# A two-layer decoder trunk on one core: sums of a Strassen weight piece queued ahead of its last two splits, and three folds of the second token tile queued behind the held weight pairs

## The chip, the cores and the metric

The kernel runs on one core of one Trainium2 chip, as one launch. The metric is device time in microseconds (us). The figure for a kernel is the median of several runs; a profiled execution has a time of its own, beside the span from its first to its last traced instruction.

## What is computed

The reference is a decoder trunk of two layers over 256 tokens of width 1024, in float32. Each layer is a half-step feed-forward block, a mixer with two gated branches, and a second half-step feed-forward block, each followed by a layer norm:

```python
def _swiglu(x, w1, w3, w2):
    return (jax.nn.silu(x @ w1) * (x @ w3)) @ w2
...
    for l in range(DEPTH):
        h = _swiglu(x, ffn_w1[l, 0], ffn_w3[l, 0], ffn_w2[l, 0])
        x = _layernorm(ALPHA * x + 0.5 * h, ln_g[l, 0], ln_b[l, 0])
        h = _mixer(x, l, w_in[l], gate_b[l], sgu_ln_g[l], sgu_ln_b[l], sgu_w[l], sgu_b[l],
                   lam[l], diff_ln_g[l], w_branch[l], w_out[l], cos, sin)
        x = _layernorm(ALPHA * x + h, ln_g[l, 1], ln_b[l, 1])
        h = _swiglu(x, ffn_w1[l, 1], ffn_w3[l, 1], ffn_w2[l, 1])
        x = _layernorm(ALPHA * x + 0.5 * h, ln_g[l, 2], ln_b[l, 2])
    return x
```

The change lies in the product with `w2` (2816 x 1024), which is done four times: twice in each of the two layers.

## The kernel before

**Tiling.** The 256 tokens are two token tiles of 128 (`t` = 0, 1), and the 1024 output columns are two halves of 512 (`c` = 0, 1). A product with a weight is kept at float32 accuracy by splitting: the weight block `raw` is copied to a rounded `hi` on ScalarE (ACT), and VectorE (DVE) makes `lo = raw - hi`; the left operand is split in the same way, and TensorE (PE) sums hi by hi, lo by hi and hi by lo (`three`, L214). So every weight block passes a chain: one transfer of 1 MB into `raw` (four buffers, issued from SP's queue), one `hi` on ACT, one `lo` on DVE (eight buffers each), then PE. A plain weight piece gives two halves of 128x1024 each (`stream`, `whi` at L172, `wlo` at L174).

**The product with w2.** The 22 row blocks of 128 of `w2` are taken in pairs. Four pairs (`SQ`) go through one Strassen step: seven products instead of eight, into seven PSUM banks `S[1]` to `S[7]`. The other seven pairs (`PQ`) are plain. The order on PE is: Strassen piece 0, plain pair, piece 1, plain pair, piece 2, plain pair, piece 3, and then four plain pairs whose splits are made but whose matmuls are held back (`held`). The held matmuls come last, for (t, c) = (0,0), (0,1), (1,0), (1,1), and within each for the four pairs in turn: 6 matmuls a pair, 24 for each (t, c).

**A Strassen piece** (`stream_s`, L284 to L319) loads one `raw` of four blocks of 512 columns. Four splits (`cut`; `shi` at L296, `slo` at L298) make the operands: `a` (512 columns, product 1), `b` (products 3 and 2), and, after sums of blocks are written back into `raw`, `c` (products 5 and 7) and `d` (products 6 and 4). The sums are three DVE instructions: L309 (1024 columns, needed by `c`), L311 and L312 (512 columns each, needed by `d`). PE takes the products in the order 1, 2, 5, 6, 3, 7, 4.

**The folds.** After piece 3 the seven products are combined and added into the residual tiles `xtok` (`ln.more`, seen as L477 and L479 on `xtok`, with `u` at L667 and `v` at L668): two adds for the first token tile (`xtok_143`: `S[1]`, `v`) and four for the second (`xtok_144`: `S[7]`, `v`, `u`, `S[7]` again). Then each held bank is added (`ln.part`, L486), followed by the statistics of the layer norm (L491, L498), the scaling of the row (L502) and PE transposes for the next stage (L546).

**What sets the order.** PE's order is written out by hand. The other engines run in order too, in the order that the scheduler of the programming layer gives them when the program is built; it goes by the order in the code, by a priority and by its own estimate of readiness. `behind(ins)` asks that an instruction is queued after a given one; `latest[1]` is the last lo split of the newest activations.

Of the kernel before, what the change touches and what calls it, by code (L numbers as in the profile page):

```python
# [17 lines left out]
ALU = mybir.AluOpType  # L18
# [38 lines left out]
def trunk(ctx, tc, x, xT, w13a, w13b, w2s, w2p, wb, wqk, wa, wbr, wo, gateb, sgug, sgub, sguwT, sgubias, lam, diffg,  # L57
          lng, lnb, lngT, lnbT, cosT, sinT, out):
    nc = tc.nc
    V, A, G, PE = nc.vector, nc.scalar, nc.gpsimd, nc.tensor  # L60
# [15 lines left out]
    def name(s):  # L76
        serial[0] += 1
        return f"{s}_{serial[0]}"
# [32 lines left out]
    def step():  # L111
        chunk[0] += 1
        tc.cur_priority = chunk[0] * STEP
# [33 lines left out]
    latest, added, emptied, silu, turned_by = [None, None], [None], [None], [None], [None]  # L147

    def behind(ins):

        return tc.issue_after(ins) if ins is not None else nullcontext()

    def stream(src, width=CH, sub=HC, lent=(), after=(None, None)):

        step()
        raw = raw_pool.tile([P, CH], F32, tag="raw", name=name("raw"))
        nc.sync.dma_start(raw[:, :width], src)
        out = []  # L160
        for o in range(0, width, HC):
            if o // HC in lent:
                hi, lo = ([act.tile([P, 512], F32R, tag="slot", name=name(n)) for _ in range(2)] for n in ("lhi", "llo"))
                at = [(hi[j], lo[j]) for j in range(2)]
            else:
                hi = hi_pool.tile([P, HC], F32R, tag="hi", name=name("whi"))
                lo = lo_pool.tile([P, HC], F32R, tag="lo", name=name("wlo"))
                at = [(hi[:, p : p + sub], lo[:, p : p + sub]) for p in range(0, HC, sub)]
            for p, (h, w) in zip(range(0, HC, sub), at):
                r = raw[:, o + p : o + p + sub]  # L170
                with behind(latest[0]):
                    A.activation(h, r, AF.Copy)  # L172
                with behind(after[o // HC] or latest[1]):
                    V.tensor_tensor(out=w, in0=r, in1=h.bitcast(F32), op=ALU.subtract)  # L174
            out.append((hi, lo))
        return out
# [78 lines left out]
    def rows_p(ps, t, q, piece, xh, xl, c0=0, n=512, stop=False, start=False):  # L255

        for j, k in enumerate(q):
            wh, wl = (v[:, j * 512 + c0 : j * 512 + c0 + n] for v in piece)
            three(ps[:, :n], xh(k)[:, t * P : (t + 1) * P], xl(k)[:, t * P : (t + 1) * P], wh, wl,
                  start and j == 0, stop and j == 1)  # L260
        beat(n / 1024)
# [21 lines left out]
    def stream_s(src, pair):  # L283

        step()
        raw = raw_pool.tile([P, CH], F32, tag="raw", name=name("raw"))
        nc.sync.dma_start(raw, src)

        def two():
            return hi_pool.tile([P, HC], F32R, tag="hi", name=name("shi")), lo_pool.tile([P, HC], F32R, tag="lo", name=name("slo"))  # L290

        def cut(p, o, n):
            h, w = (v[:, p[2] : p[2] + n] for v in p[:2])
            r = raw[:, o : o + n]
            with behind(latest[0]):
                A.activation(h, r, AF.Copy)  # L296
            with behind(latest[1]):
                V.tensor_tensor(out=w, in0=r, in1=h.bitcast(F32), op=ALU.subtract)  # L298

        a = (*pair, 0) if pair else None  # L300
        if a is None:
            pair = two()
            a, keep = (*pair, 0), pair
        else:
            a, keep = (*pair, 512), None
        b, c, d = ((*two(), 0) for _ in range(3))
        cut(a, 0, 512)
        cut(b, 1024, 1024)
        V.tensor_tensor(out=raw[:, :1024], in0=raw[:, :1024], in1=raw[:, 512:1536], op=ALU.add)  # L309
        cut(c, 0, 1024)  # L310
        V.tensor_tensor(out=raw[:, 1024:1536], in0=raw[:, :512], in1=raw[:, 1024:1536], op=ALU.add)  # L311
        V.tensor_tensor(out=raw[:, 1536:], in0=raw[:, 1024:1536], in1=raw[:, 1536:], op=ALU.add)  # L312
        cut(d, 1024, 1024)

        def at(p, j):
            return tuple(v[:, p[2] + j * 512 : p[2] + j * 512 + 512] for v in p[:2])

        return keep, {1: at(a, 0), 3: at(b, 0), 2: at(b, 1), 5: at(c, 0), 7: at(c, 1), 6: at(d, 0), 4: at(d, 1)}
# [246 lines left out]
    def ffn(l, f, i, norm, last=False):  # L565
# [77 lines left out]
        pair, held, plain = None, [], list(PQ)  # L643

        def plain_pair(hold):
            q = plain.pop(0)
            w = stream(w2p[l, f, PQ.index(q)])
            if hold:
                held.append((q, w))
                return  # L650
            for c in range(2):
                for t in range(NT):
                    for ps, o, m in ends[t, c]:
                        rows_p(ps, t, q, w[c], hh, hl, o, m, start=q == PQ[0] and t + c == 2)

        for n, q in enumerate(SQ):
            pair, w = stream_s(w2s[l, f, n], pair)
            for b in (1, 2, 5, 6, 3, 7, 4):
                three(S[b], *s_op[q][b], *w[b], n == 0, n == NS - 1 and b in (1, 5, 6, 7))
            beat(1.75)  # L660
            if n < NS - 1:
                plain_pair(False)
# [4 lines left out]
        V.tensor_tensor(out=u, in0=u, in1=S[1], op=ALU.add)  # L667
        V.tensor_tensor(out=v, in0=S[5], in1=u, op=ALU.subtract)  # L668
        ln.more(0, 1, v, ALU.add, ln.scale)
        ln.more(1, 1, v, ALU.add, ln.scale)  # L670
        ln.more(1, 0, u, ALU.add)
        ln.more(1, 1, S[7], ALU.add)
        while plain:
            plain_pair(True)
        for t in range(NT):
            for c in range(2):
                for ps, o, n in ends[t, c]:
# [230 lines left out]
    for l in range(DEPTH):  # L908
        norm = ffn(l, 0, 0, norm)
        norm = mixer(l, 1, norm)  # L910
        norm = ffn(l, 1, 2, norm, last=l == DEPTH - 1)
# [89 lines left out]
```

## Time and profile before

| | |
|---|---|
| median of 3 runs | 1233.25 us (1232.46 to 1234.97) |
| the profiled execution: time, span | 1233.15 us, 1231.4 us |
| DVE busy | 935.2 us (76%) |
| ACT busy | 804.0 us (65%) |
| POOL busy | 87.3 us (7%) |
| bytes moved | 252.28 MB, mean 205 GB/s |
| ACT `shi` L296 waiting for DVE `raw` L312 | 39.1 us in 16 waits |
| DVE `slo` L298 waiting for ACT `shi` L296 | 27.5 us in 21 waits |

The share of busy time is a mean over all stages. PE matmuls are pipelined: one of 512 columns has a recorded duration of some 390 ns, while the next starts some 227 ns after it, so PE time is read from the distance between starts, and a stall is a distance that is longer. Idle time of DVE or ACT costs something only where PE then waits.

### The profile page before, as it was taken

What the parts mean: (1) busy time and instruction counts of PE and PEld (TensorE: products, weight loads), DVE (VectorE), ACT (ScalarE), POOL (GpSimd) and SP (SyncE); (2) the same over time, 40 slices, a digit from 0 to 9 for tenths busy, and PEclk for the clock granted to TensorE, in tenths of its full rate; (3) what the DMA queues carried; (4) which work ended last, traced back from release to release, by engine and by line L of the source; (5) the groups of instructions that cost most, each with busy time, mean ns of one, the idle gap of its engine ahead of it and who ended that gap; (6) DMA issues with size and microseconds to landing.
All of it is one profiled execution on the core that took longest, in us unless ns stands there. A gap on an engine that the chain in (4) does not pass through costs nothing.

```text
span 1231.4 us, 16550 instructions
## 1 busy us (share of the span) xinstructions
PE 1215.8 (99%) x6045; PEld 1022.6 (83%) x6045; DVE 935.2 (76%) x1504; ACT 804.0 (65%) x1316; POOL 87.3 (7%) x184
## 2 busy tenths in 40 slices
PE   9999999999999999999999999999999999999997
PEld 8888878888888888888788888788888888888885
DVE  6657997886587985679974779979767879657795
ACT  6677666679665565776556776467885654776760
POOL 0100000234100000000000000002440000000000
PEclk9999999999999999999999999999999999999999
DMA  8985665654744657666756756565556356668540
GB/s 316 315 260 175 236 238 175 212 173 161 258 173 151 239 178 249 202 176 227 251 176 234 209 184 239 205 216 189 177 185 226 138 190 222 224 198 240 172 173 35
DMA packets 82338, 252.28 MB, mean 205 GB/s; under 512 B 47521, under 2 KB 48593, under 8 KB 55633
## 3 DMA queue, kind: packets, MB, share of 16 engines
q1 hardware_dynamic: 78288, 238.31, 57.5%
q0 software_dynamic: 3536, 12.13, 3.0%
q8 instruction: 47, 0.77, 0.2%
q10 hardware_dynamic: 432, 0.79, 0.2%
q14 instruction: 35, 0.28, 0.1%
HBM read 235.47 MB, written 1.05 MB: 192 GB/s over the span
## 4 chain that ended last, share of the span: by engine, by line
PE 58%; issue 22%; DVE 12%; ACT 5%; DMA 2%; POOL 1%; DVEq 0%; ACTq 0%; POOLq 0%
PE bank L214 19%; PE sbank L214 16%; PE bank L226 12%; PE bank L233 6%; DVE wlo L174 3%; DVE slo L298 3%; PE bank L385 2%; ACT shi L296 1%; ACT columns L601 1%; PE sbank L734 1%; DVE xtok L479 1%; ACT whi L172 1%; DVE raw L312 1%; DMA bc<-in_lng 1%; DVE hlo L180 1%
## 5 line engine op out<-in xcount | busy, mean ns | idle before, releaser
L174 DVE TENSOR_TENSOR wlo<-raw,whi 128x1024 fp32r<-128x1024 f32 (+1 forms) x410 | 450.7, 1117 | 161.6 <-ACT whi L172 118.0
L172 ACT ACTIVATE whi<-raw 128x1024 fp32r<-128x1024 f32 (+1 forms) x410 | 387.0, 968 | 192.5 <-PE sbank L214 67.9
L214 PE MATMUL bank<-whi,x 128*128 128x512 f32 x840 | 264.7, 391 | 0.0
L214 PEld LDWEIGHTS bank<-whi,x 128*128 128x128 f32 x840 | 157.8, 188 | 32.5
L214 PE MATMUL bank<-wlo,x 128*128 128x512 f32 x420 | 163.6, 390 | 0.0
L214 PE MATMUL sbank<-whi,x 128*128 128x512 f32 x512 | 158.9, 389 | 0.0
L226 PE MATMUL bank<-x,whi 128*128 128x512 f32 x640 | 158.4, 396 | 0.0
L226 PEld LDWEIGHTS bank<-x,whi 128*128 128x128 f32 x640 | 116.6, 188 | 25.9 <-issue 2.6
L214 PEld LDWEIGHTS sbank<-whi,x 128*128 128x128 f32 x512 | 96.1, 188 | 19.9
L214 PE MATMUL sbank<-wlo,x 128*128 128x512 f32 x256 | 99.7, 389 | 0.0
L296 ACT ACTIVATE shi<-raw 128x1024 fp32r<-128x1024 f32 (+1 forms) x64 | 58.9, 945 | 56.9 <-DVE raw L312 39.1
L214 PEld LDWEIGHTS bank<-wlo,x 128*128 128x128 f32 x420 | 78.9, 188 | 16.0
L298 DVE TENSOR_TENSOR slo<-raw,shi 128x1024 fp32r<-128x1024 f32 (+1 forms) x64 | 68.8, 1088 | 27.5 <-ACT shi L296 27.5
L233 PE MATMUL bank<-x,wlo 128*128 128x256 f32 x640 | 85.8, 285 | 0.0
L233 PEld LDWEIGHTS bank<-x,wlo 128*128 128x128 f32 x640 | 81.5, 191 | 2.3
L214 PE MATMUL sbank<-whi,hhi 128*128 128x512 f32 x168 | 66.4, 395 | 0.0
L214 PE MATMUL sbank<-wlo,hhi 128*128 128x512 f32 x168 | 66.2, 394 | 0.0
L214 PE MATMUL sbank<-whi,hlo 128*128 128x512 f32 x168 | 66.0, 393 | 0.0
L234 ACT ACTIVATE r<-bank 128x256 f32<-128x256 f32 x112 | 41.8, 379 | 27.6 <-PE bank L233 27.6
L552 ACT ACTIVATE xf<-sbank,ln_b,ln_g 128x128 f32<-128x128 f32 x80 | 30.0, 455 | 40.8 <-PE sbank L546 40.8
L214 PEld LDWEIGHTS sbank<-wlo,x 128*128 128x128 f32 x256 | 48.1, 188 | 10.0
L445 POOL DMA_DIRECT2D bc<-in_lng x6 | 3.2, 530 | 712.9 <-DVE bc L444 712.9
(233 smaller groups left out, 1938.7 us busy)
## 6 DMA issues: line engine op xcount, KB each, us to landing
raw<-in_w13b SPq DMA_DIRECT2D x76, 1024.0 KB, 5.4
raw<-in_w2p SPq DMA_DIRECT2D x28, 1024.0 KB, 4.9
raw<-in_wa SPq DMA_DIRECT2D x24, 1024.0 KB, 5.3
raw<-in_w2s SPq DMA_DIRECT2D x16, 1024.0 KB, 4.9
raw<-in_wb SPq DMA_DIRECT2D x16, 1024.0 KB, 4.9
raw<-in_wqk SPq DMA_DIRECT2D x16, 1024.0 KB, 4.8
raw<-in_wbr SPq DMA_DIRECT2D x16, 1024.0 KB, 4.8
raw<-in_w13a SPq DMA_DIRECT2D x8, 1024.0 KB, 4.8
```

The costliest lines, as they stand in the source:

```text
L172: A.activation(h, r, AF.Copy)
L174: V.tensor_tensor(out=w, in0=r, in1=h.bitcast(F32), op=ALU.subtract)
L180: return a.ins, V.tensor_tensor(out=lo, in0=src, in1=hi.bitcast(F32), op=ALU.subtract).ins
L214: PE.matmul(ps, xx, w, start=start and n == 0, stop=stop and n == 2)
L226: PE.matmul(b[-1], hi[:, k * P : (k + 1) * P], xc(k), start=k == 0, stop=False)
L233: PE.matmul(b[n][:, :T], lo[:, k * P : (k + 1) * P], xc(k)[:, :T], start=False, stop=k == KT - 1)
L234: emptied[0] = A.activation(r[:, s], b[n][:, T:], AF.Copy, scale=scale).ins
L296: A.activation(h, r, AF.Copy)
L298: V.tensor_tensor(out=w, in0=r, in1=h.bitcast(F32), op=ALU.subtract)
L312: V.tensor_tensor(out=raw[:, 1536:], in0=raw[:, 1024:1536], in1=raw[:, 1536:], op=ALU.add)
L385: PE.matmul(ps[t][m], x[:, j, o + t * P : o + (t + 1) * P], y, start=k0 + j == 0 and o == 0 and y is hi, stop=k0 + j == KT - 1 and y is lo)
L552: A.activation(xf[:, s], b[:, s], AF.Identity, scale=self.gT[:, f], bias=self.bT[:, f])
```

## The change

Two places are written in another order. In `stream_s` the three sums are all written ahead of the splits `c` and `d`, and both lo splits of these two are asked to be queued behind the last sum. In `ffn` the loop that streams the four held pairs is written ahead of the last three folds of the second token tile. No instruction is added or removed, and the arithmetic is the same.

```diff
-        def cut(p, o, n):
+        def cut(p, o, n, after=None):
             h, w = (v[:, p[2] : p[2] + n] for v in p[:2])
             r = raw[:, o : o + n]
             with behind(latest[0]):
                 A.activation(h, r, AF.Copy)
-            with behind(latest[1]):
+            with behind(after or latest[1]):
                 V.tensor_tensor(out=w, in0=r, in1=h.bitcast(F32), op=ALU.subtract)
...
         V.tensor_tensor(out=raw[:, :1024], in0=raw[:, :1024], in1=raw[:, 512:1536], op=ALU.add)
-        cut(c, 0, 1024)
         V.tensor_tensor(out=raw[:, 1024:1536], in0=raw[:, :512], in1=raw[:, 1024:1536], op=ALU.add)
-        V.tensor_tensor(out=raw[:, 1536:], in0=raw[:, 1024:1536], in1=raw[:, 1536:], op=ALU.add)
+        last = V.tensor_tensor(out=raw[:, 1536:], in0=raw[:, 1024:1536], in1=raw[:, 1536:], op=ALU.add).ins
+        cut(c, 0, 1024, last)
         cut(d, 1024, 1024)
...
         ln.more(0, 1, v, ALU.add, ln.scale)
+        while plain:
+            plain_pair(True)
         ln.more(1, 1, v, ALU.add, ln.scale)
         ln.more(1, 0, u, ALU.add)
         ln.more(1, 1, S[7], ALU.add)
-        while plain:
-            plain_pair(True)
```

In the built program PE's order and the queues of SP and POOL are unchanged; DVE's order changes, and ACT's in two kinds of places.

On DVE, in piece 3 of the first of the four products with `w2`, the rows run before as follows; `slo_1438` is the lo of split `b`, `slo_1440` of `c`, `slo_1442` of `d`, and L311 and L312 are the two sums that `d` needs.

```order
L298 TENSOR_TENSOR slo_1438<-raw_1435,shi_1437 128x1024
L298 TENSOR_TENSOR slo_1440<-raw_1435,shi_1439 128x1024
L311 TENSOR_TENSOR raw_1435<-raw_1435 128x512
L312 TENSOR_TENSOR raw_1435<-raw_1435 128x512
L298 TENSOR_TENSOR slo_1442<-raw_1435,shi_1441 128x1024
```

The same place after the change (in the new line numbers the two sums are L310 and L311):

```order
L298 TENSOR_TENSOR slo_1438<-raw_1435,shi_1437 128x1024
L310 TENSOR_TENSOR raw_1435<-raw_1435 128x512
L311 TENSOR_TENSOR raw_1435<-raw_1435 128x512
L298 TENSOR_TENSOR slo_1440<-raw_1435,shi_1439 128x1024
L298 TENSOR_TENSOR slo_1442<-raw_1435,shi_1441 128x1024
```

The lo split of `c` now stands behind the two sums, directly ahead of that of `d`. Pieces 0 and 1 change alike; in piece 2 the scheduler had other work between these rows, and only their order changes.

Next on DVE come the folds and the splits of the held pairs. Before, from the end of the first fold group to the first held bank; `wlo_1513` is the second half of the third held pair, `wlo_1519` and `wlo_1523` are the two halves of the fourth:

```order
L668 TENSOR_TENSOR v_1476<-bank_1206,u_1475 128x512
L477 TENSOR_TENSOR xtok_144<-xtok_144,u_1475 128x512
L479 SCALAR_TENSOR_TENSOR xtok_143<-xtok_143,v_1476 128x512
L479 SCALAR_TENSOR_TENSOR xtok_144<-xtok_144,v_1476 128x512
L174 TENSOR_TENSOR wlo_1513<-raw_1506,whi_1512 128x1024
L477 TENSOR_TENSOR xtok_144<-xtok_144,sbank_1202 128x512
L174 TENSOR_TENSOR wlo_1519<-raw_1516,whi_1518 128x1024
L174 TENSOR_TENSOR wlo_1523<-raw_1516,whi_1522 128x1024
L174 TENSOR_TENSOR llo_1704<-raw_1700,lhi_1702 128x512
L486 TENSOR_TENSOR xtok_143<-xtok_143,bank_1205 128x512
```

The same place after, where the same three halves are `wlo_1510`, `wlo_1516` and `wlo_1520`:

```order
L668 TENSOR_TENSOR v_1476<-bank_1206,u_1475 128x512
L174 TENSOR_TENSOR wlo_1510<-raw_1503,whi_1509 128x1024
L479 SCALAR_TENSOR_TENSOR xtok_143<-xtok_143,v_1476 128x512
L174 TENSOR_TENSOR wlo_1516<-raw_1513,whi_1515 128x1024
L174 TENSOR_TENSOR wlo_1520<-raw_1513,whi_1519 128x1024
L479 SCALAR_TENSOR_TENSOR xtok_144<-xtok_144,v_1476 128x512
L477 TENSOR_TENSOR xtok_144<-xtok_144,u_1475 128x512
L477 TENSOR_TENSOR xtok_144<-xtok_144,sbank_1202 128x512
L486 TENSOR_TENSOR xtok_143<-xtok_143,bank_1205 128x512
```

Three of the four folds that stood ahead of the fourth pair's first half now stand behind its second half. The other three products with `w2` change in the same way.

On ACT, in piece 1 of the fourth product, the rows before are these; `shi_11169` is the hi of `d`, `whi_11205` and `whi_11209` those of the plain pair behind it, and L464 scales the norm's row of gains once, for the last norm only:

```order
L296 ACTIVATE shi_11169<-raw_11163 128x1024
L464 ACTIVATE bc_11067<-bc_11067 128x1024
L172 ACTIVATE whi_11205<-raw_11203 128x1024
L172 ACTIVATE whi_11209<-raw_11203 128x1024
L296 ACTIVATE shi_11239<-raw_11237 128x512
```

After the change they are these:

```order
L296 ACTIVATE shi_11169<-raw_11163 128x1024
L172 ACTIVATE whi_11205<-raw_11203 128x1024
L172 ACTIVATE whi_11209<-raw_11203 128x1024
L464 ACTIVATE bc_11067<-bc_11067 128x1024
L296 ACTIVATE shi_11239<-raw_11237 128x512
```

The scaling has moved behind the plain pair's two hi copies.

## The prediction

> **What bounds the kernel now.** I read the engines' busy time first, then what PE waited for.
>
> ```profile
> span 1231.4 us, 16550 instructions
> PE 1215.8 (99%) x6045; PEld 1022.6 (83%) x6045; DVE 935.2 (76%) x1504; ACT 804.0 (65%) x1316; POOL 87.3 (7%) x184
> ...
> PE bank L214 <- DVE wlo L174: 9.0, 4, 3.2
> ```
>
> PE is busy for 99% of the span, and nearly all its recorded waiting is one thing, four times, once in each product with `w2`: a matmul waits for the lo split of a weight. So an edit can only pay by what it takes from these four waits. The timeline of PE shows the first of them and the last:
>
> ```profile
> 165.22 0.39 PE L214 MATMUL bank<-whi,hlo 128*128 128x512 f32 x1
> 165.45 0.39 PE L214 MATMUL bank<-whi,hhi 128*128 128x512 f32 x1
> 167.75 0.50 PE L214 MATMUL bank<-wlo,hhi 128*128 128x512 f32 x1 [1.92 <-DVE wlo L174]
> 168.09 0.40 PE L214 MATMUL bank<-whi,hlo 128*128 128x512 f32 x1
> ...
> 1199.85 0.39 PE L214 MATMUL bank<-whi,hhi 128*128 128x512 f32 x1
> 1203.44 0.50 PE L214 MATMUL bank<-wlo,hhi 128*128 128x512 f32 x1 [3.21 <-DVE wlo L174]
> 1203.78 0.39 PE L214 MATMUL bank<-whi,hlo 128*128 128x512 f32 x1
> ...
> 1204.71 0.56 PE L214 MATMUL sbank<-whi,hhi 128*128 128x512 f32 x1
> ...
> 1208.35 0.40 PE L214 MATMUL sbank<-whi,hhi 128*128 128x512 f32 x1
> ```
>
> Undisturbed starts lie 0.227 us apart (165.22 to 165.45). The first wait stretches two such steps to 168.09 - 165.45 = 2.64 us, a loss of 2.19, which is the idle 1.92 and 0.27 more (pipelining given up, and one slower step). The last one loses 3.93 - 0.45 = 3.48, again idle plus 0.27. All four lose 9.0 + 4 x 0.27 = 10.1 us. The last has an aftermath: nine steps from 1204.71 to 1208.35 take 3.64 us instead of 2.04. The stretches by window show why (busy times of PE, PEld, DVE, ACT, POOL, then the granted clock, DMA share and GB/s):
>
> ```profile
> 168.00:172.00 4.00, 4.00 (x19) 3.27 (x19) 4.00 (x7) 0.00 (x0) 0.00 (x0) 1.00 0.95 375
> ...
> 1204.70:1208.10 3.40, 3.40 (x10) 2.62 (x9) 1.44 (x3) 0.00 (x0) 0.00 (x0) 0.51 0.00 0
> ```
>
> After the idle 3.21 the clock was granted at 0.51, after the idle 1.92 at 1.00. That is 1.60 us more. Together 11.7 us hang on four splits.
>
> By the Trainium skill, "TensorE: Matmul & The Clock Gate", Part 1, "What's actually happening", the array falls to half its clock after an idle window of about 3.4 us. The trace fell at 3.21 idle, so read strictly the page would not blame this wait for the 1.60 and would leave it in the time; the row decides here, and the strict reading is a rival below.
>
> **What DVE does ahead of that split.** The split waited for is the first half of the fourth held pair. DVE's timeline in the first product:
>
> ```profile
> 162.35 0.68 DVE L668 TENSOR_TENSOR v<-bank,u 128x512 f32<-128x512 f32 x1
> 162.95 0.68 DVE L477 TENSOR_TENSOR xtok<-xtok,u 128x512 f32<-128x512 f32 x1
> 163.55 1.29 DVE L479 SCALAR_TENSOR_TENSOR xtok<-xtok,v 128x512 f32<-128x512 f32 x2
> 164.75 1.22 DVE L174 TENSOR_TENSOR wlo<-raw,whi 128x1024 fp32r<-128x1024 f32 x1
> 165.88 0.68 DVE L477 TENSOR_TENSOR xtok<-xtok,sbank 128x512 f32<-128x512 f32 x1
> 166.48 2.35 DVE L174 TENSOR_TENSOR wlo<-raw,whi 128x1024 fp32r<-128x1024 f32 x2
> ```
>
> The last row holds both halves of the fourth pair; the first ends at 166.48 + 1.22 = 167.70, and PE goes on at 167.75. PE wanted it at 165.45 + 0.23 = 165.68. Ahead of it, behind `v`, stand four folds, one each 0.60 us from start to start.
>
> **Term 1, the folds.** One of the four stays ahead, three go behind the pair: 3 x 0.60 = 1.80 earlier, an end at 165.90. That alone leaves PE 0.22 late.
>
> **Term 2, the sums.** The end of a Strassen piece, DVE and then ACT:
>
> ```profile
> 148.85 2.35 DVE L298 TENSOR_TENSOR slo<-raw,shi 128x1024 fp32r<-128x1024 f32 x2
> 151.12 0.68 DVE L311 TENSOR_TENSOR raw<-raw 128x512 f32<-128x512 f32 x1
> 151.83 0.69 DVE L312 TENSOR_TENSOR raw<-raw 128x512 f32<-128x512 f32 x1
> 153.73 1.23 DVE L298 TENSOR_TENSOR slo<-raw,shi 128x1024 fp32r<-128x1024 f32 x1 [1.21 <-ACT shi L296]
> ...
> 152.64 1.06 ACT L296 ACTIVATE shi<-raw 128x1024 fp32r<-128x1024 f32 x1 [4.45 <-DVE raw L312]
> ```
>
> The first row is the lo of `b` and of `c`; the latter starts at 149.98. After the second sum DVE stands idle 1.21 while ACT makes the hi of `d`. With the sums first, they start at 149.98 and 150.70 and end at 151.39; ACT follows after the same 0.12 as now, from 151.51 to 152.57, beside the lo of `c` (151.30 to 152.52); the lo of `d` starts at 152.60 instead of 153.73. So DVE comes 1.13 earlier to the held pairs. Not all of it arrives, because a fold of product 1 and the second pair's hi lie between, and these follow PE:
>
> ```profile
> 157.06 0.39 PE L214 MATMUL bank<-shi,shl 128*128 128x512 f32 x1
> ...
> 158.19 0.39 PE L214 MATMUL bank<-slo,shh 128*128 128x512 f32 x1
> ...
> 158.28 0.68 DVE L479 SCALAR_TENSOR_TENSOR xtok<-xtok,bank 128x512 f32<-128x512 f32 x1
> ...
> 156.86 2.01 ACT L172 ACTIVATE whi<-raw 128x1024 fp32r<-128x1024 f32 x2 [0.32 <-PE sbank L214]
> ...
> 160.26 2.96 ACT L172 ACTIVATE whi<-raw 128x1024 fp32r<-128x1024 f32 x3
> ```
>
> Product 1 ends at 157.06 + 0.39 = 157.45, so its fold can start at about 157.5, 0.78 earlier than 158.28; the next hi (156.86 + 1.06 = 157.92) is ready for the split at 158.1. The hi of the fourth pair comes second in the last row, at about 162.3, before DVE can take it (163.9). Term 2 is thus worth 0.78, between 0 (were the fold to stay) and 1.13. The awaited split ends at 167.70 - 1.80 - 0.78 = 165.12, 0.56 before PE asks. The first wait goes whole, and the second and third, which have the same rows and idle (9.0 - 1.92 - 3.21 = 3.87 for both), go too.
>
> **The last product** is further behind:
>
> ```profile
> 1169.56 1.23 DVE L298 TENSOR_TENSOR slo<-raw,shi 128x1024 fp32r<-128x1024 f32 x1 [1.19 <-ACT shi L296]
> 1171.68 2.36 DVE L174 TENSOR_TENSOR wlo<-raw,whi 128x1024 fp32r<-128x1024 f32 x2 [0.89 <-ACT whi L172]
> ...
> 1193.97 0.68 DVE L479 SCALAR_TENSOR_TENSOR xtok<-xtok,bank 128x512 f32<-128x512 f32 x1
> ...
> 1202.17 2.35 DVE L174 TENSOR_TENSOR wlo<-raw,whi 128x1024 fp32r<-128x1024 f32 x2
> ...
> 1191.46 0.39 PE L214 MATMUL bank<-shi,shl 128*128 128x512 f32 x1
> ...
> 1169.64 1.06 ACT L464 ACTIVATE bc<-bc 128x1024 f32<-128x1024 f32 x1
> ```
>
> The awaited half ends at 1202.17 + 1.22 = 1203.39, and PE asks at 1199.85 + 0.23 = 1200.08: 3.31 to make up. The folds give 1.80, piece 3 gives 1.13 (product 1 ends at 1191.46 + 0.39, so its fold at 1193.97 could move by 2.1), together 2.93, and 0.38 is missing. In piece 1 the sums take away the idle 1.19 too, and L464, which stands ahead of the hi that DVE awaits at 1171.68, moves behind it; either covers 0.38, since DVE has hardly a pause from there to the held pairs, and the transfer into the buffer that piece 1 frees starts earlier with it. If neither reached the held pairs, the end would be 1200.46, and PE would lose 0.38, the 0.05 from the split's end to PE, and one slower step of 0.11: 0.54 us. I take 0. An idle of 0.4 is far under 1.92, so the slow clock goes as well.
>
> **What is delayed.** The lo of `c` goes behind both sums, 1.32 later. In the piece shown it ends at 152.52, and product 5, the first to read it, reads at 158.19: 5.7 us of cover. Without cover it would cost PE up to 1.32 in each of 16 pieces. The three folds (1.80) now stand ahead of the first held bank's add and statistics. The next place where DVE and PE meet is the second bank:
>
> ```profile
> 174.66 0.69 DVE L486 TENSOR_TENSOR xtok<-xtok,sbank 128x512 f32<-128x512 f32 x1 [1.02 <-PE sbank L214]
> 178.41 1.00 DVE L502 TENSOR_SCALAR xtok<-xtok,mv,nwy 128x512 f32<-128x512 f32 x2
> 181.26 0.60 PE L546 MATMUL sbank<-ident,xtok 128*128 128x128 f32 x4
> ```
>
> PE brings it 2.19 earlier, at 172.47. DVE, free at 173.64 now, gains 0.78 and has one 0.60 split fewer ahead of it: 172.26, in time by 0.2. That split then stands between the add and the statistics and delays the scaling by about 0.5 against PE; scaling to transposes has 181.26 - 179.41 = 1.85. No transfer starts later: SP's order is the same, and each issue waits for a DVE split that comes earlier.
>
> **The sum.** 10.1 + 1.6 = 11.7 us off the span of 1231.4 gives 1219.7. The profiled execution took 1233.15, 1.75 outside the span, so 1221.5; it lies 0.1 under the median of 1233.25. Forecast for the median: 1221.6 us.
>
> **The rivals.** *Only the folds count*: something else holds the split at its place and term 2 is 0. Then PE loses 0.22 + 0.05 + 0.11 three times, and in the last product 1203.39 - 1.80 - 1200.08 = 1.51 + 0.16, together 2.8: 1224.4 us. For it speaks that 0.35 of term 2 is already lost to product 1; against it that nothing else stands there. *The slow clock has another cause* (the strict reading above) and returns at its place: 1221.6 + 1.6 = 1223.2; against it speaks that it follows the longest wait within 1.3 us and none of the others. *The wait moves*: DVE, with three folds in hand, is late for the second bank and the transposes wait; the margins of 0.2 and 1.85 speak against it. If it ate the gain of the three products that have a next stage (3 x 2.2), 1228.2; for no change the last product's 5.1 must be lost as well. *Slower*: the lo of `c` is late in the Strassen pieces. At no cover 16 x 1.32 = 21.1 us is lost, 1242.7 us; it decides from 11.7 / 16 = 0.73 us lost per piece, where the cover read is 5.7.
>
> **How the numbers follow.** Forecast, with up to 0.5 left in the last product: 0.73. Only the folds: 0.11. Slow clock stays: 0.03. The wait moves: 0.08, of which 0.03 as far as no change. Late `c`: 0.03. Two further in a hundred are for a slower run by what I do not see. A change under 0.2% (2.5 us) is about what these runs cannot tell from none. Faster: 0.73 + 0.11 + 0.03 + 0.05 = 0.92; same 0.03; slower 0.05. The range goes from 1220.0, twice as far under the forecast as the lowest run of the kernel before lies under its median (0.8), to 1225.0, which takes in folds alone.
>
> **What would show it.** Right: PE has no wait for `wlo` in the four held stages, the granted clock stays at 1.00 behind the last, ACT waits for the sums less long, and DVE's 1.21 ahead of `slo` shrinks to about 0.1. Wrong: a PE wait at the same matmul of some 0.3 (term 2 fails), waits ahead of L546 (the wait moved), or ahead of a matmul on `slo`.

## The result, and the profile after

The changed kernel took 1221.16 us, the median of four runs (1221.10 to 1221.18). The kernel before took 1233.99 (1232.46 to 1234.97); that is the median of four runs, the three of the table and one more. The ratio is 0.990, with a 95% interval from 0.9888 to 0.9912: faster by 12.8 us. The forecast was 1221.6. Between the two profiled executions, 1233.15 and 1221.16, the difference is 12.0 us; the other 0.8 is scatter of the kernel before, which its four runs show and the four of the changed kernel don't.

The first lines of the changed kernel's page, and below them all the waits of PE in its trace (sum, count and longest):

```profile
span 1219.2 us, 16555 instructions
PE 1212.0 (99%) x6045; PEld 1020.6 (84%) x6045; DVE 934.9 (77%) x1504; ACT 806.2 (66%) x1316; POOL 87.8 (7%) x184
...
PE sbank L397 <- DVE warm L393: 1.0, 1, 1.0
PE sbank L514 <- DVE xtok L493: 1.0, 1, 1.0
PE bank L385 <- ACT whi L179: 0.5, 1, 0.5
PE sbank L518 <- ACT minus L516: 0.2, 1, 0.2
```

The 9.0 us for `wlo` are gone, and what is left comes to 2.7 us. PE's timeline at the two matmuls that waited, in the first product and in the last:

```profile
164.69 0.39 PE L214 MATMUL bank<-whi,hlo 128*128 128x512 f32 x1
164.92 0.39 PE L214 MATMUL bank<-whi,hhi 128*128 128x512 f32 x1
165.15 0.39 PE L214 MATMUL bank<-wlo,hhi 128*128 128x512 f32 x1
165.37 0.39 PE L214 MATMUL bank<-whi,hlo 128*128 128x512 f32 x1
...
1192.63 0.39 PE L214 MATMUL bank<-whi,hhi 128*128 128x512 f32 x1
1192.86 0.39 PE L214 MATMUL bank<-wlo,hhi 128*128 128x512 f32 x1
```

The step onto the `wlo` matmul now takes 0.23 us like every other; before, it took 2.30 in the first product (165.45 to 167.75) and 3.59 in the last (1199.85 to 1203.44). The DVE timeline of the same place, in the first product and in the last:

```profile
161.03 0.68 DVE L668 TENSOR_TENSOR v<-bank,u 128x512 f32<-128x512 f32 x1
161.63 1.22 DVE L174 TENSOR_TENSOR wlo<-raw,whi 128x1024 fp32r<-128x1024 f32 x1
162.77 0.69 DVE L479 SCALAR_TENSOR_TENSOR xtok<-xtok,v 128x512 f32<-128x512 f32 x1
163.37 2.36 DVE L174 TENSOR_TENSOR wlo<-raw,whi 128x1024 fp32r<-128x1024 f32 x2
165.64 0.69 DVE L479 SCALAR_TENSOR_TENSOR xtok<-xtok,v 128x512 f32<-128x512 f32 x1
...
1184.67 0.69 DVE L479 SCALAR_TENSOR_TENSOR xtok<-xtok,bank 128x512 f32<-128x512 f32 x1 [0.89 <-PE bank L214]
...
1191.08 2.36 DVE L174 TENSOR_TENSOR wlo<-raw,whi 128x1024 fp32r<-128x1024 f32 x2
```

The awaited split ends at 163.37 + 1.22 = 164.59, and PE asks at 165.15: 0.56 us to spare. In the last product it ends at 1191.08 + 1.22 = 1192.30, and PE asks at 1192.86: 0.56 again. The four products read alike (0.56 each). Behind the last of them the granted clock (third number from the end) stays at 1.00:

```profile
1180.00:1219.00 39.00, 33.60 (x143) 26.26 (x141) 27.70 (x50) 8.52 (x12) 0.73 (x2) 1.00 0.16 55
```

The span fell by 12.2 us where 11.7 were argued. The other 0.5 us is won before any instruction that the change touches, as the timeline of the first matmuls shows, before and after:

```profile
5.32 1.82 PE L385 MATMUL bank<-whi,x 128*128 128x512 f32 x4
...
7.44 1.08 PE L385 MATMUL bank<-whi,x 128*128 128x512 f32 x4
```

```profile
5.46 1.18 PE L385 MATMUL bank<-whi,x 128*128 128x512 f32 x4 [0.55 <-ACT whi L179]
...
6.93 1.07 PE L385 MATMUL bank<-whi,x 128*128 128x512 f32 x4
```

The same four matmuls take 1.82 us in one execution and 1.18 in the other, and two groups later PE is 0.51 ahead. It keeps this to 164.92 against 165.45. The traces' record of the granted clock says what differs: the clock first rises to 1.00 at 6.70 us in the one and at 4.49 in the other. Over all ten traces of this document, a rise that comes 1.38, 1.23, 0.78 or 0.67 us after these four matmuls start goes with 1.82, 1.74, 1.54 and 1.49 us for them (the kernel before, the lo of `c` behind that of `d`, the sums alone, one fold ahead); a rise before their start, or within 0.1 us behind it, goes with 1.18 to 1.23. Kernels that hold the whole change or most of it stand on both sides. So these 0.5 us belong to the moment at which the clock rises in an execution, and not to the change: this part of the result is luck. The profiled execution took 1221.16, 1.96 more than its span; before, the difference was 1.75.

### The profile page after: what moved, and what is told of

Its sections match the earlier page's. It is cut to its first block, busy times and chain, and to the rows that moved or that the text cites. A ratio compares the mean times of both kernels' runs of the same rounds, so it can differ in the third digit from the quotient of the medians.

```text
span 1219.2 us, 16555 instructions
## 1 busy us (share of the span) xinstructions
PE 1212.0 (99%) x6045; PEld 1020.6 (84%) x6045; DVE 934.9 (77%) x1504; ACT 806.2 (66%) x1316; POOL 87.8 (7%) x184
## 4 chain that ended last, share of the span: by engine, by line
PE 99%; DMA 0%; DVE 0%; ACT 0%; DVEq 0%; issue 0%; ACTq 0%
PE bank L214 37%; PE sbank L214 26%; PE bank L226 17%; PE bank L233 9%; PE sbank L226 2%; PE bank L385 2%; PE sbank L233 1%; PE sbank L734 1%; PE sbank L546 1%; PE sbank L783 1%; PE sbank L864 1%; DMA xraw<-in_xT 0%; PE sbank L781 0%; PE sbank L805 0%; PE sbank L768 0%; PE sbank L773 0%
## 5 line engine op out<-in xcount | busy, mean ns | idle before, releaser
L298 DVE TENSOR_TENSOR slo<-raw,shi 128x1024 fp32r<-128x1024 f32 (+1 forms) x64 | 69.3, 1088 | 14.4 <-ACT shi L296 13.7
```

## The experiments

They ask four things: what each half of the change is worth, what PE loses per us of lateness, how much cover the lo of `c` has, and what the slow clock hangs on. For each kernel the trace gives the margin, which is the time at which PE asks for the fourth pair's first lo half less the time at which that half is done. Diffs are against the changed kernel.

**The folds alone.** The sums stand where they stood before:

```diff
+        cut(c, 0, 1024)
         V.tensor_tensor(out=raw[:, 1024:1536], in0=raw[:, :512], in1=raw[:, 1024:1536], op=ALU.add)
-        last = V.tensor_tensor(out=raw[:, 1536:], ...).ins
-        cut(c, 0, 1024, last)
+        V.tensor_tensor(out=raw[:, 1536:], ...)
```

> The three folds go behind the held pairs, the sums stay in their old order. Theory (both halves of the change are needed; the cost is the lateness of the fourth pair's first lo split plus 0.16 us): the split is 2.02 - 1.80 = 0.22 late in the first three products, a loss of 0.38 each, and 3.31 - 1.80 = 1.51 late in the last, a loss of 1.67 at an undiminished clock; 2.8 us in all, 1224.0 us against 1221.16. Rival (the folds alone do it, the sums bring nothing): 1221.2. Rival (the sums alone do it): 1233.

Measured: 1223.96 us (1223.86 to 1224.14), a ratio of 0.9923 (0.9909 to 0.9938) to the kernel before on that chip (1233.16). PE's timeline in the first product:

```profile
164.67 0.39 PE L214 MATMUL bank<-whi,hhi 128*128 128x512 f32 x1
165.20 0.50 PE L214 MATMUL bank<-wlo,hhi 128*128 128x512 f32 x1
```

The step takes 0.53 instead of 0.23. Margins: -0.24, -0.24, -0.22 and -1.65; the losses of PE are 0.42, 0.42, 0.41 and 1.86. This is the prediction's rival "only the folds count" (1224.4), and it was the right price for this half. In the last product the half is 1.65 late where 1.51 was priced.

**The sums alone.** The three folds stand ahead of the held pairs, as before:

```diff
-        while plain:
-            plain_pair(True)
         ln.more(1, 1, v, ALU.add, ln.scale)
         ln.more(1, 0, u, ALU.add)
         ln.more(1, 1, S[7], ALU.add)
+        while plain:
+            plain_pair(True)
```

> The sums go first, the folds stay ahead of the held pairs. Theory: the split comes 0.78 earlier than before in the first three products (held there by the fold of product 1), so it is 1.24 late, a loss of 1.40 each; in the last it comes up to 2.1 earlier, 1.2 late, a loss of 1.37; no slow clock. 5.6 us in all, 1226.8 us. Rival (the sums bring nothing): 1232.5 to 1234. Rival (the sums alone do it): 1221.2.

Measured: 1226.87 us (1226.64 to 1227.26), ratio 0.9947 (0.9932 to 0.9962). The same place on PE:

```profile
165.13 0.39 PE L214 MATMUL bank<-whi,hhi 128*128 128x512 f32 x1
166.66 0.50 PE L214 MATMUL bank<-wlo,hhi 128*128 128x512 f32 x1 [1.14 <-DVE wlo L174]
```

The margin is -1.24 in all four products, the last included, and each loses 1.43. So the sums are worth 2.03 - 1.24 = 0.79 in the first product, where the prediction had 0.78, and 3.32 - 1.24 = 2.08 in the last. Neither half takes the waits away alone.

**Part of the folds.** Of the three folds, one stands ahead of the pairs again, then two; and last, the fold that the change left ahead goes behind as well. The first of the three edits:

```diff
+        ln.more(1, 1, v, ALU.add, ln.scale)
         while plain:
             plain_pair(True)
-        ln.more(1, 1, v, ALU.add, ln.scale)
```

> As the changed kernel, but one of its three folds stands ahead of the fourth pair again. The trace of the changed kernel has the awaited split 0.56 ahead of PE in all four products; one fold takes 0.60. Theory (only the lateness of that split counts, and slack is free up to its end): 0.04 late, a loss of 0 to 0.2 in each product, 1221.2 to 1222.0 us. Rival (every fold ahead costs its 0.60): 4 x 0.60 more, 1223.6.

> As the changed kernel, but two of its three folds stand ahead of the fourth pair again. Theory: 1.20 - 0.56 = 0.64 late, a loss of 0.64 + 0.16 = 0.80 in each product, 1224.4 us. Rival (every fold ahead costs its 0.60): 4.8 more, 1226.0.

> As the changed kernel, but the fold of the first token tile goes behind the held pairs too, so that four stand there. Theory: the split is 1.16 ahead of PE instead of 0.56, and nothing waits for it: 1221.2 us as before the edit. Rival (the wait moves): with four folds in hand DVE comes 0.6 later to the second held bank than now, and the norm behind it delays PE's transposes in three products, up to 0.6 each: 1223.

Measured, beside 1232.68 for the kernel before: 1222.06 (1221.71 to 1222.34), ratio 0.9912 (0.9897 to 0.9927); 1224.46 (1224.13 to 1225.79), 0.9934 (0.9919 to 0.9948); and 1221.20 (1220.91 to 1221.51), 0.9906 (0.9889 to 0.9922). PE with one fold ahead, then with two:

```profile
164.94 0.39 PE L214 MATMUL bank<-whi,hhi 128*128 128x512 f32 x1
165.26 0.50 PE L214 MATMUL bank<-wlo,hhi 128*128 128x512 f32 x1
```

```profile
164.86 0.39 PE L214 MATMUL bank<-whi,hhi 128*128 128x512 f32 x1
165.78 0.50 PE L214 MATMUL bank<-wlo,hhi 128*128 128x512 f32 x1 [0.54 <-DVE wlo L174]
```

The margins are -0.04, -0.64 and +1.16, that is the 0.56 less 0.60, less 1.20 and plus 0.60. Losses per product are 0.23, 0.84 and 0. Put in a row with the other kernels:

| kernel | margin, us | loss per product, us |
|---|---|---|
| all folds behind | +1.16 | 0 |
| the change | +0.56 | 0 |
| one fold ahead | -0.04 | 0.23 |
| folds alone | -0.24 | 0.42 |
| two folds ahead | -0.64 | 0.84 |
| sums alone | -1.24 | 1.43 |
| before, first three products | -2.03 | 2.21 |

The loss is the lateness and about 0.2 us more. Four times the loss, put on the changed kernel's 1221.16, gives 1222.1, 1224.5 and 1226.9 for one fold, two folds and the sums alone: what was measured, within 0.1. For the folds alone the four losses come to 3.1 and give 1224.3, 0.3 above the measured 1223.96; in that trace PE was 0.25 us ahead of the changed kernel before the first loss (164.67 against 164.92). Slack beyond zero, the fourth fold behind, buys nothing.

**The lo of `c` behind that of `d`.** It stands still later, which takes the disputed cover to its end:

```diff
-        cut(c, 0, 1024, last)
-        cut(d, 1024, 1024)
+        for p, o in ((c, 0), (d, 1024)):
+            with behind(latest[0]):
+                A.activation(p[0], raw[:, o : o + 1024], AF.Copy)
+        for p, o in ((d, 1024), (c, 0)):
+            with behind(last):
+                last = V.tensor_tensor(out=p[1], ..., op=ALU.subtract).ins
```

> As the changed kernel, but the lo split of c is queued behind that of d, some 2.3 later in piece 3 than in the changed kernel; the operands are the same. Theory: product 5 reads it some 5.7 after its end in the changed kernel, so PE does not notice, and DVE's later arrival is covered by its idle time ahead of the fold of product 1: 1221.2 us. Rival (the lo of c has little cover, so that queueing it behind the sums already uses it up): up to 1 us lost in each of 16 pieces, 1230 and more.

Measured: 1222.08 us (1221.42 to 1222.32), ratio 0.9911 (0.9897 to 0.9926), a miss of 0.9 us. DVE at the end of piece 3 of the first product; L317 is both splits, `d` first:

```profile
150.59 0.69 DVE L311 TENSOR_TENSOR raw<-raw 128x512 f32<-128x512 f32 x1
152.49 2.36 DVE L317 TENSOR_TENSOR slo<-raw,shi 128x1024 fp32r<-128x1024 f32 x2 [1.21 <-ACT shi L314]
...
158.17 0.68 DVE L483 SCALAR_TENSOR_TENSOR xtok<-xtok,bank 128x512 f32<-128x512 f32 x1
```

The rival, a late `c`, did not come: its lo ends at 152.49 + 2.36 = 154.85, product 5 first reads it at 158.15 in this run, and PE has no wait on `slo`. What the expectation overlooked is the idle 1.21: with `d` first, DVE again has nothing to do while ACT makes the hi of `d`, in 12 places (13.7 us in all). The fold of product 1 starts at 158.17, no longer held by PE, and the margins are -0.16, -0.16, -0.17 and +0.31. The first three cost 0.34 us each, 1.0 in all, which is the miss. So the order of the two splits is a working part of the change: the lo of `c` fills the time that ACT needs.

**The slow clock, in the last product alone.** The first three products are as changed. In the last one the sums are old, and three of the folds stand ahead of the pairs; in the second kernel two:

```diff
+        if not first:          # in the last product alone, ahead of the last two sums
+            cut(c, 0, 1024)
...
-        cut(c, 0, 1024, last)
+        if first:              # in the other three, behind them
+            cut(c, 0, 1024, last)
...
+        ahead = 3 if last else 0   # second kernel: 2 if last else 0
+        for fold in folds[:ahead]:
+            fold()
         while plain:
             plain_pair(True)
-        ln.more(...)  # the three
+        for fold in folds[ahead:]:
+            fold()
```

> The change is made in the first three products with w2 only; the last one is as before. Theory: the last wait returns with idle 3.2, a loss of 3.48, and with it the clock of 0.51 behind it, 1.60: 1226.2 us. Rival (the slow clock has another cause than this wait, and went for another reason): 1224.6.

> As the run with the last product as before, but there one of the three folds goes behind the held pairs. Theory: the split is 3.31 - 0.60 = 2.71 late, idle 2.6, a loss of 2.87. If the clock falls only after an idle between 2.6 and 3.2, it stays at 1.00 and the time is 1224.0 us; if it falls somewhere between 1.93 and 2.6, the time is about 1225.6 with some 3 us at 0.5 behind the wait.

Measured with three ahead: 1225.37 us, scattered over 1224.31, 1224.69, 1226.05 and 1226.61, ratio 0.9933 (0.9917 to 0.995). With two ahead: 1225.23 (1224.97 to 1225.37), ratio 0.9933 (0.9919 to 0.9948). PE's waits show what was set up, first with three ahead, then with two:

```profile
PE bank L214 <- DVE wlo L174: 3.2, 1, 3.2
```

```profile
PE bank L214 <- DVE wlo L174: 2.6, 1, 2.6
```

One profiled run of each kernel shows the slow clock at its wait (1226.05 and 1224.97 us). The other runs left only a time and a mean clock. A mean of 1.000 leaves no room for such a stretch, since 3.41 us at 0.50 take 0.0014 off. A mean of 0.999 alone doesn't prove one, because the half clock behind the last matmul counts too: with two folds ahead in every product it is 0.999 without a slow stretch before 1220.46. With three ahead, the runs of 1224.31 and 1224.69 have a mean of 1.000, that of 1226.61 has 0.999: by this the larger wait brought the slow clock in two runs of four, and each of its two expectations came true in half the runs. With two ahead, the means are 0.998 and 0.999 and all times lie within 0.4 us of the profiled run, so the smaller wait probably brought it in all four. The length of the wait does not decide it alone. The windows at these places (length, busy PE, PEld, DVE, ACT, POOL, then granted clock, DMA share, GB/s), in the kernel before, with three folds ahead and with two:

```profile
163.71:167.12 3.41, 2.12 (x10) 1.43 (x8) 3.41 (x5) 3.07 (x6) 0.00 (x0) 1.00 0.29 91
167.12:170.53 3.41, 2.77 (x12) 2.32 (x13) 3.41 (x5) 0.00 (x0) 0.00 (x0) 1.00 0.92 315
...
1201.37:1204.78 3.41, 1.34 (x6) 1.12 (x7) 3.16 (x4) 0.00 (x0) 0.00 (x0) 1.00 0.02 5
1204.78:1208.19 3.41, 3.41 (x10) 2.64 (x9) 1.44 (x3) 0.00 (x0) 0.00 (x0) 0.50 0.00 0
```

```profile
1193.22:1196.63 3.41, 0.49 (x2) 0.45 (x3) 3.41 (x4) 0.00 (x0) 0.00 (x0) 1.00 0.00 0
1196.63:1200.04 3.41, 3.41 (x10) 2.64 (x9) 2.03 (x4) 0.00 (x0) 0.00 (x0) 0.50 0.02 5
```

```profile
1191.60:1195.01 3.41, 1.10 (x5) 0.56 (x3) 3.41 (x5) 0.00 (x0) 0.00 (x0) 1.00 0.00 0
1195.01:1198.42 3.41, 3.11 (x7) 2.48 (x8) 2.55 (x4) 0.00 (x0) 0.00 (x0) 0.50 0.02 5
```

The slow stretch is 3.41 us each time, and in each trace it starts a whole number of 3.413 us steps after the clock first rose (351, 349 and 349 steps). Read on this grid, a step in which PE was busy for 1.34, 1.10 or 0.49 us was followed by one at half clock; after steps with 2.12 and 2.77 us the clock stayed at 1.00. A wait that falls across a boundary leaves PE busy in both steps, and the first wait of the kernel before did (167.12 lies inside it). Once the clock has risen, this holds without exception in all ten traces: every step with up to 1.34 us was followed by half clock, none with 1.43 or more was. The two nearest to the bound stand at the ends of runs, behind other matmuls: with one fold ahead, then with the lo of `c` behind that of `d`:

```profile
1214.15:1217.56 3.41, 1.43 (x4) 0.55 (x4) 1.98 (x5) 0.00 (x0) 0.00 (x0) 1.00 0.33 122
1217.56:1220.08 2.52, 0.00 (x0) 0.00 (x0) 0.00 (x0) 0.00 (x0) 0.00 (x0) 1.00 0.15 50
...
1214.90:1218.31 3.41, 1.26 (x4) 0.38 (x2) 1.84 (x4) 0.00 (x0) 0.00 (x0) 1.00 0.38 141
1218.31:1220.20 1.89, 0.00 (x0) 0.00 (x0) 0.00 (x0) 0.00 (x0) 0.00 (x0) 0.50 0.11 33
```

The Trainium skill, "TensorE: Matmul & The Clock Gate", Part 1, "What's actually happening", says that the clock follows a free-running window of 3413 ns; these traces agree (3.41 us, on a fixed grid). It gives an idle window as the condition for half clock; here windows with 0.49 to 1.34 us of work were enough.

## Why the prediction was right, point by point

- **The four waits.** Predicted gone, with 0.56 us to spare in the first product; measured 0.56. The folds' 1.80 is shown by the steps of 0.60 in the table, the sums' 0.78 by 0.79 (sums alone) and 0.80 (0.56 + 0.24, folds alone). The bound that made it 0.78 and not 1.13, that the fold of product 1 waits for PE, is in the trace below.
- **The last product.** It needed 3.31 and the terms from folds and piece 3 gave 2.93; the prediction took the missing 0.38 as covered by the pieces ahead. Shown: the sums alone moved it by 2.08, far beyond piece 3's 1.13, and the change stopped at 0.56 because DVE now waits 0.89 for PE ahead of the fold at 1184.67. So what arrived beyond piece 3 came from ahead of it. In piece 1 and the plain pair behind it, DVE's waits of 1.19 ahead of `slo` and 0.89 ahead of `wlo` are gone, and one of 0.58 ahead of a split between the sums of piece 2 is new. How much of that the sums gave and how much moving L464 gave was not tried; in these kernels L464 moves whenever the sums do.
- **The end of a piece.** DVE in piece 3 of the first product, then the held stage's meetings with PE:

```profile
148.24 0.69 DVE L310 TENSOR_TENSOR raw<-raw 128x512 f32<-128x512 f32 x1
148.97 0.69 DVE L311 TENSOR_TENSOR raw<-raw 128x512 f32<-128x512 f32 x1
149.57 2.52 DVE L298 TENSOR_TENSOR slo<-raw,shi 128x1024 fp32r<-128x1024 f32 x2
152.01 2.36 DVE L174 TENSOR_TENSOR wlo<-raw,whi 128x1024 fp32r<-128x1024 f32 x2
154.70 1.23 DVE L174 TENSOR_TENSOR wlo<-raw,whi 128x1024 fp32r<-128x1024 f32 x1 [0.33 <-ACT whi L172]
...
156.96 0.69 DVE L479 SCALAR_TENSOR_TENSOR xtok<-xtok,bank 128x512 f32<-128x512 f32 x1 [1.03 <-PE bank L214]
...
171.92 0.69 DVE L486 TENSOR_TENSOR xtok<-xtok,sbank 128x512 f32<-128x512 f32 x1 [0.19 <-PE sbank L214]
```

The splits of `c` and `d` are one row of 2.52 us, two halves of 1.22 and less than 0.1 between: the idle 1.21 ahead of `d` is gone, as said. The fold of product 1 waits 1.03 for PE, which is the bound on term 2. At the second held bank DVE is in time by 0.19, where 0.2 was said, and PE's list has no wait ahead of the transposes (L546), so the rival of a wait that moves is out. On ACT, the 16 waits for the last sum fell from 39.1 us to the first row (those for the first sum, L309, rose from 0.8 to 4.4), and DVE's waits for the hi from 27.5 us in 21 to the second:

```profile
ACT shi L296 <- DVE raw L311: 23.8, 16, 3.1
...
DVE slo L298 <- ACT shi L296: 13.7, 10, 2.3
```

- **The late `c`.** PE has no wait on `slo`, not even with `c` behind `d`, where 3.3 us of cover were left in piece 3 of the first product (158.15 - 154.85): that rival is out, by a wide margin.
- **Mis-sized: a small wait.** For lateness of a few tenths the prediction took 0.16 us on top, 0.05 from the split's end to PE and 0.11 for one slower step. The table shows 0.2. With one fold ahead the half is late by 0.04, PE goes on 0.09 late (165.26 for 165.17), and after the slower step it is 0.23 behind, so that its 1222.06 lies just above the 1222.0 that was the most expected. It counted only in the rivals: "folds alone" loses 0.42 + 0.42 + 0.41 + 1.86 = 3.1 us in its trace, where the prediction had 2.8; that its time lay so near the price is in part the early start of its execution.
- **Right by luck: the slow clock's condition.** The prediction read it as a matter of how long PE is idle, 1.92 or 3.21. The 1.60 us was the right size for the profiled execution, and without waits it is gone. With the last wait put back, the profiled run has the slow stretch again, and the four runs of the changed kernel, with a mean clock of 1.000, have none, so the rival of another cause is out. But a wait of 2.6 suffices, and one of 3.2 brought it, by times and mean clocks, in half the runs. Part of the scatter of the kernel before, 1232.35 to 1234.97 in the three series, may go with this: in the two series beside the experiments, its runs of 1234.14 to 1234.43 us have mean clocks of 0.997, those of 1232.35 to 1233.6 have 0.998 and 0.999. Whether the slower ones have a second slow stretch is not shown, since they have no profile.

## What to carry to other kernels

When the bound engine stops for one late operand, list what the producing engine does ahead of it that nobody needs yet, and see how far each item can move before it meets the bound engine somewhere else: in the first product 1.80 and 0.78 us arrived of 1.80 and 1.13. Two moves that each leave the operand late can take the whole wait only together, and slack beyond that is worth nothing. Where an engine waits for a partner, put a piece of work that is already possible into the gap rather than behind it; the same two splits in the other order brought the gap back.

## What was not expected of the hardware

- At each of these waits, with the operand from 0.04 to 3.3 us late, PE lost about 0.2 us on top of the lateness; margins around zero are worth clearing.
- The clock's drop to one half lasts 3.41 us and comes on a fixed grid of 3.413 us steps. In the ten traces it goes with how much of the step before PE was busy (up to 1.34 us: it drops; 1.43 and more: it stays). Runs of one kernel, with three folds ahead in the last product, differed by 1.4 to 2.3 us, in step with their mean clocks; 3.41 us at half clock can take at most 1.7 of that, and the moment of the first rise moved the start by up to 0.6 between traces (1.82 against 1.18).
